# The FFN's entrance of an encoder layer: five instead of three pairs of gate and up tiles form their first four products ahead of the token sums

## The chip, the cores and the metric

The kernel runs on one core of a Trainium2 chip. The metric is the device time of one execution in microseconds (us), lower is better. A run's time is the median of several executions of the same program.

## The reference

One layer of a hybrid encoder on 1024 tokens of 1024 channels, float32 throughout. An attention group and a memory (mLSTM) group share an input and an output projection; then comes the feed-forward part (FFN), in which the change lies:

```python
    x = x + g1[:, None, :] * mix
    h = modulate(rms_norm(x, norm_ffn_g[l]), sh2, sc2)
    ffn = (jax.nn.silu(h @ w_gate[l]) * (h @ w_up[l])) @ w_down[l]
    x = x + g2[:, None, :] * ffn
return rms_norm(x, final_norm_g)
```

`w_gate` and `w_up` are 1024 x 2816, `w_down` is 2816 x 1024.

## The kernel before

**Products in split precision.** TensorE multiplies float32r operands, so each float32 operand is cut into a high part (ScalarE, ACT: a copy that rounds) and a low part (the rest, a subtraction on VectorE, DVE, or GpSimd, POOL). One product of a 128-row weight tile with a block of the tokens is four groups (`k`) of three matmuls each (`mm3`, L310): weight high with tokens high, weight high with tokens low, weight low with tokens high. All of them are 128x128 by 128x512. In the profile `whi` and `wlo` are the weight's parts, and `h110h`, `h213l`, `hT20h` and the like the tokens'; the low parts of the token sums overwrite tiles of the residual stream and are called `x` there.

**Seven products in place of eight.** The gate and up projections run by a scheme of the Strassen-Winograd kind. The hidden rows come in 11 pairs `p` (`NP`), and each pair has a gate tile (`i` = 0) and an up tile (`i` = 1). Weights and tokens are cut into 2 x 2 blocks. For each pair and each `i` there are seven products, named by what multiplies the tokens: `"11"`, `"21"`, `"22"`, `"T2"`, `"T3"`, `"T1"`, `"T4"`. Blocks `"11"` and `"21"` are the second half of the tokens as it is, normed. Block `"22"` is a block of the first half. The `T` blocks are **token sums**: chains of additions over all four blocks (`sums` in `norm2`, L1391), for four `k` each, almost all on DVE.

**What runs when.** `FF` is the order of units on TensorE:

```python
FF = [("b", p) for p in range(NB)] + [("v", 0)] + [("s", (p, i)) for p in range(1, NP - 1) for i in range(2)] + [("v", NP - 1)]
```

A unit `b` (`first_unit`, L1545) forms the first four products of pair `p`: `"11"` for gate and up, and `"21"` for gate and up. They need no token sums. A unit `v` (`pair_unit`, L1593) forms a pair's other ten products, gate and up in turn, with `"22"` first for pair 0. A unit `s` (`set_unit`, L1610) forms the other products of one tile: five where `p < NB`, and all seven where `p >= NB`. Before, units `b` stand for pairs 0, 1 and 2.

**What a product's bank is emptied by.** Each product fills one of the eight PSUM banks. The `"11"` product is copied out by ACT (`keep`, L1509). The `"21"` product is added to that copy by DVE (`c11`, L1526); for the gate tile a SiLU on ACT follows, for the up tile a multiplication on DVE (`post`, L1518) and a store. Their tiles come from `gu_tile` (L1498): pair 0 takes them from the rings `sg` and `su`, pairs 1 and 2 from tiles left over from the norm (`gsq`, `gssq`, `gv`, `gy`, and `gu`). For pair 2, `c11` also waits until the last mean has been multiplied in (`rs_used`).

**Weights.** A weight piece is loaded by a DMA from SyncE's queue (SP) into one of three `wst` tiles (`raw`, L442), then split; there are six `whi` and six `wlo` tiles (`wp`). Product n's end asks for piece n + 6 (`load_piece`, L487). Plain pieces of pair 0 have their low part made by DVE, those of later units `b` by POOL. The sums of weights for the other five products (`S1` to `S4`, and `A22`) come from raw tiles `wr` (three for each tile, `load_raws`, L1429) and one more `wst` (`load_last`, L1439). Their low part is DVE's for pair 0, POOL's for all others (`set_piece`, L1448). `load_last` for pair 0 is called in the unit `b` of pair `NB - 2`.

**Who sets the order.** The order of instructions on every engine is written out by a planner in the kernel (`Clock`), which runs its own estimate of the time. It lets a product start only when the bank taken eight allocations earlier has been given back in its own estimate (`slot`, L336); which bank the product really gets is settled later. The mean of the squares of the first token half takes one such bank (`ms`, L1342) and gives it back after eight multiplications with it (`normed`, L1364). The engines then work through their queues in that order, each waiting on semaphores.

Of the kernel before, what the change touches and what calls it, by code (L numbers as in the profile page):

```python
# [11 lines left out]
F32 = mybir.dt.float32  # L12
# [8 lines left out]
P = 128  # L21
# [3 lines left out]
HALF = 512  # L25
# [14 lines left out]
NX = 2  # L40
WARM = 4
PES = 3
NB = 3
KB = 5
AHEAD = 2
NP = NF // 2
# [2 lines left out]
MIX = [("o", i) for i in range(16)] + [("m", (i + 8) % 16) for i in range(16)]  # L49
FF = [("b", p) for p in range(NB)] + [("v", 0)] + [("s", (p, i)) for p in range(1, NP - 1) for i in range(2)] + [("v", NP - 1)]  # L50
SET = ["A11", "A12", "S2", "S3", "S1", "A22", "S4"]
# [198 lines left out]
def layer_kernel(ctx, tc, xT, c, w_ada, vecs, cons, rope, w_f, w_fT, w_t0, w_t, w_o, w_gu, w_d, out):  # L250
# [113 lines left out]
    with tc.manual_schedule():  # L364
# [41 lines left out]
        def set_w(p, i):  # L406
            return [("set", (p, i, m)) for m in SET if p >= NB or m not in ("A11", "A12")]

# [1030 lines left out]
        def load_last(s):  # L1439
            p, i = divmod(s, 2)  # L1440

            def arrived(t, delay):
                RAW[s]["12"][0] = t
                ck.chain(delay, lambda: None, flag=RAW[s]["12"][1])

            raw([P, 4, P], gate_w(p, i, 0, 1), sets_done[s], arrived)

        def set_piece(e, p, i, m):  # L1448
# [16 lines left out]
            else:  # L1465
                split(e, 0.0, lambda: R["12"][0], sh, s2_ok[s], R["12"][1], *done("A12"),
                      lambda: dve.tensor_sub(R["12"][0], R["12"][0], Q[2]), lo=eng)
            if len(set_p[s]) == (7 if p >= NB else 5):
                ck.chain(0.0, *set_p[s].values(), lambda: None, flag=sets_done[s])
# [17 lines left out]
        def prod(idx, m):  # L1487

            for k in range(4):
                yield [pieces[idx][2], hb_ok[m, k]] + ([slot("acc")] if k == 0 else [])  # L1490
                if k == 0:
                    bank = psum_tile([P, HALF], "acc")
                mm3(bank[0], weights(idx, k, 4), HB[m, k], k == 0, k == 3)
                ck.pe(0.65)
            load_piece()
            return bank

        def gu_tile(p, i, m):  # L1498
            if p == 2 and m in ("11", "12"):
                if i:  # L1500
                    return fp.tile([P, HALF], F32, name="gu")
                tag = "v" if m == "12" else "y"
                return NPL[0].tile([P, HALF], F32, tag=tag, name="g" + tag)
            if p == 1 and m in ("11", "12"):
                tag = "ssq" if i else "sq"
                return NPL[0].tile([P, HALF], F32, tag=tag, name="g" + tag, bufs=2 - i)
            return fp.tile([P, HALF], F32, tag=("sg", "su")[i], name=("sg", "su")[i], bufs=(6, 4)[i])

        def keep(p, i, X):  # L1509
            e = U[p, i] = [None, X[1]]  # L1510

            def copy():
                e[0] = gu_tile(p, i, "12")
                act.activation(e[0], X[0], AF.Copy)

            ck.chain(LAT, copy, flag=X[1])
# [9 lines left out]
        def c11(p, i, X):  # L1526
            u, u_ok = U[p, i]
            T = []

            def add():  # L1530
                T.append(fp.tile([P, HALF], F32, tag="tt", name="c11", bufs=4) if i else gu_tile(p, 0, "11"))
                dve.tensor_add(T[0], X[0], U[p, i][0])

            ck.chain(LAT, u_ok, *(rs_used if p == 2 else ()), add, flag=X[1])
            ck.chain(0.0, X[1], lambda: post(p, i, "11", T[0], FREE))
            if i:
                ck.chain(0.0, a_ok[p, "11"], lambda: store_act(p, "11", SG[p]["11"]))
            return X[1]
# [6 lines left out]
        def first_unit(p, w0):  # L1545
            for i in range(2):
                keep(p, i, (yield from prod(w0 + i, "11")))
            for i in range(2):
                if p == NB - 2:
                    load_last(i)  # L1550
                C11[p, i] = c11(p, i, (yield from prod(w0 + 2 + i, "21")))

        def set_steps(p, i):
# [3 lines left out]
            def add(out, a, b):  # L1557
                if out not in T:
                    T[out] = gu_tile(p, i, out)
                dve.tensor_add(T[out], a[0], T[b])  # L1560
# [32 lines left out]
        def pair_unit(p, w0):  # L1593

            if p >= NB:
                for i in range(2):
# [13 lines left out]
        def set_unit(pi, w0):  # L1610
            p, i = pi
            if p >= NB:
                keep(p, i, (yield from prod(w0, "11")))
# [609 lines left out]
        fp = ffpool.__enter__()  # L2223
# [90 lines left out]
```

## Time and profile before

| | us |
|---|---|
| median of 3 runs (lowest, highest) | 1393.42 (1390.51, 1393.83) |
| the profiled execution's own time | 1393.51 |
| its span, first to last instruction | 1391.7 |
| TensorE busy | 1289.2 (93%) |
| DVE busy | 1033.3 (74%) |
| ACT busy | 709.0 (51%) |
| POOL busy | 706.1 (51%) |

All times in the views count from the span's start. The stage around the change runs from about 714 us (first product of pair 0) to about 791 us (last product of `v` of pair 0). From there to 1160 us run the units of the other pairs, then the down projection. In the timeline a row is an instruction, or several alike merged: start, duration, engine, line, operation, output and inputs, count, and in brackets the idle time ahead of it with what ended it. Nearly all instructions of ACT, DVE and POOL have line L98, since one helper records them, so groups go by their tiles. Matmul durations overlap: the distance from start to start is what a matmul costs.

### The profile page before, as it was taken

Reading aid. Unit: us, or ns where it says so; the run is one execution under the profiler, and the core shown is the slowest. Engines: PE = TensorE matmul, PEld = TensorE weight load, DVE = VectorE, ACT = ScalarE, POOL = GpSimd, SP = SyncE. Lnnn points to the kernel's source line nnn. Section 1 sums busy time; section 2 is a strip of 40 time slices with the busy share of each in tenths; the row PEclk is TensorE's granted clock in tenths of the full one; section 3 lists DMA queues with packets and bytes.
Section 4 is the critical chain, followed back from the end, with each engine's and each line's share of the span. In section 5 each row is a group of like instructions: output and inputs, shape, how many; then the busy total and the mean of one; then the engine's idle time right before and its main releaser. Section 6 shows DMA issues by size and latency. Waiting matters only on the chain.

```text
span 1391.7 us, 19566 instructions
## 1 busy us (share of the span) xinstructions
PE 1289.2 (93%) x6588; PEld 1079.7 (78%) x6596; DVE 1033.3 (74%) x1536; ACT 709.0 (51%) x1335; POOL 706.1 (51%) x584
## 2 busy tenths in 40 slices
PE   7898888899999979989997899999999999979997
PEld 5786677888778978777776788888888887857887
DVE  6936698975789747758689886766676654998866
ACT  6575366778577755454477333332333334344462
POOL 0344677655656525677512265554554545445542
PEclk9999999999999999999999899999999999989999
DMA  9444433233233235663652343233332259733324
GB/s 355 158 129 118 114 103 95 84 99 105 65 108 97 67 131 180 201 225 102 198 187 89 105 138 106 99 107 106 114 114 81 76 178 328 288 79 103 95 64 155
DMA packets 103892, 185.98 MB, mean 134 GB/s; under 512 B 11504, under 2 KB 33136, under 8 KB 103792
## 3 DMA queue, kind: packets, MB, share of 16 engines
q1 hardware_dynamic: 90400, 162.63, 36.8%
q10 hardware_dynamic: 13392, 22.10, 4.2%
q8 instruction: 52, 0.85, 0.2%
q14 instruction: 48, 0.39, 0.1%
HBM read 137.76 MB, written 43.25 MB: 130 GB/s over the span
## 4 chain that ended last, share of the span: by engine, by line
PE 55%; DVE 18%; issue 8%; DMA 6%; ACT 5%; POOL 5%; SPq 1%; DVEq 0%; POOLq 0%; ACTq 0%
PE acc L311 15%; PE acc L312 15%; PE acc L313 15%; DVE sst L98 3%; DVE y L98 2%; DVE PT L98 2%; PE av L1209 2%; DVE x L98 2%; PE T L1190 2%; POOL wlo L98 2%; PE S L1158 1%; SPq L316 1%; DMA x<-in_xT_dram 1%; PE acct L313 1%; DVE s L98 1%
## 5 line engine op out<-in xcount | busy, mean ns | idle before, releaser
L98 POOL TENSOR_TENSOR wlo<-wst,whi 128x512 fp32r<-128x512 f32 (+2 forms) x187 | 264.5, 1420 | 262.3 <-ACT whi L98 236.4
L98 ACT ACTIVATE whi<-wst 128x512 fp32r<-128x512 f32 (+2 forms) x219 | 131.0, 605 | 110.2 <-PE acc L313 34.2
L312 PE MATMUL acc<-x,whi 128*128 128x512 f32 x352 | 138.4, 393 | 5.9 <-DVE x L98 5.9
L98 POOL TENSOR_SCALAR P<-P,sst 128x1024 f32<-128x1024 f32 x64 | 85.1, 1330 | 88.1 <-DVE sst L98 64.3
L98 POOL TENSOR_TENSOR wlo<-wr,whi 128x512 fp32r<-128x512 f32 x56 | 77.4, 1383 | 76.9 <-ACT whi L98 75.5
L311 PE MATMUL acc<-hh,whi 128*128 128x512 f32 x224 | 97.8, 436 | 6.5 <-ACT xp L98 5.3
L311 PE MATMUL acc<-whi,wch 128*128 128x512 f32 x244 | 96.5, 395 | 6.1 <-ACT wch L98 6.1
L313 PE MATMUL acc<-whi,wcl 128*128 128x512 f32 x244 | 96.8, 397 | 2.9 <-DVE wcl L98 2.8
L312 PE MATMUL acc<-wlo,wch 128*128 128x512 f32 x244 | 96.1, 394 | 0.1
L98 ACT ACTIVATE P<-S,sst,colq 128x1024 f32<-128x1024 f32 x64 | 77.2, 1207 | 36.8 <-DVE sst L98 26.9
L98 ACT ACTIVATE whi<-wr 128x512 fp32r<-128x512 f32 x60 | 37.9, 632 | 107.5 <-DVE wr L98 50.1
L98 DVE TENSOR_TENSOR PT<-T,PT 128x512 fp32r<-128x512 f32 x128 | 83.3, 681 | 10.7 <-ACT PT L98 10.5
L312 PE MATMUL acc<-hl,whi 128*128 128x512 f32 x224 | 90.9, 406 | 0.0
L313 PE MATMUL acc<-hh,wlo 128*128 128x512 f32 x224 | 90.8, 405 | 0.0
L98 POOL TENSOR_TENSOR wlo<-s,whi 128x512 fp32r<-128x512 f32 x40 | 54.0, 1352 | 67.5 <-ACT whi L98 67.5
L1190 PE MATMUL T<-ident,P 128*128 128x128 f32 x512 | 72.8, 280 | 15.9 <-DVE PT L98 9.3
L98 DVE TENSOR_TENSOR sg<-acc,sg 128x512 f32<-128x512 f32 x67 | 45.4, 687 | 55.8 <-PE acc L313 55.5
L311 PE MATMUL acct<-whi,hh 128*128 128x256 f32 (+1 forms) x256 | 82.8, 324 | 4.2 <-ACT hh L98 2.8
L98 ACT ACTIVATE PT<-T 128x512 fp32r<-128x512 f32 x128 | 71.8, 596 | 28.5 <-PE T L1190 27.8
L98 DVE TENSOR_REDUCE sst<-S 128x1 f32<-128x1024 f32 x64 | 77.7, 1214 | 11.4 <-PE S L1158 9.9
L312 PEld LDWEIGHTS acc<-x,whi 128*128 128x128 f32 x352 | 66.5, 189 | 21.0 <-DVE x L98 7.3
L98 POOL TENSOR_TENSOR ada<-ada,cond 128x512 f32<-128x512 f32 x48 | 69.2, 1443 | 23.3 <-DMA ada<-in_w_ada_dram 23.2
(478 smaller groups left out, 3859.6 us busy)
## 6 DMA issues: line engine op xcount, KB each, us to landing
wr<-in_w_gu_dram SPq DMA_DIRECT2D x66, 256.0 KB, 2.7
ada<-in_w_ada_dram SPq DMA_DIRECT2D x64, 256.0 KB, 3.2
wd<-in_w_d_dram SPq DMA_DIRECT2D x22, 512.0 KB, 6.4
wst<-in_w_gu_dram SPq DMA_DIRECT2D x34, 256.0 KB, 3.1
wst<-act_d SPq DMA_DIRECT2D x33, 256.0 KB, 4.1
ada<-in_w_ada_dram SPq DMA_DIRECT2D x16, 512.0 KB, 7.1
wst<-in_w_o_dram SPq DMA_DIRECT2D x32, 256.0 KB, 3.9
act_d<-sg ACTq DMA_DIRECT2D x31, 256.0 KB, 2.2
```

Source lines behind the costliest of these rows:

```text
L98: return fn(*args, **kw)
L311: nc.tensor.matmul(acc, w[0], x[0], start=first, stop=False)
L312: nc.tensor.matmul(acc, w[0], x[1], start=False, stop=False)
L313: nc.tensor.matmul(acc, w[1], x[0], start=False, stop=last)
L316: (q or nc.sync).dma_start(dst, src)
L1158: nc.tensor.matmul(sp[:, halves(n)], qs[:, j * P:(j + 1) * P], k2[g][m][:, halves(n)], start=m == 0, stop=m == 1)
L1190: nc.tensor.transpose(tp[:, k], Pt[q][:, (4 * b + k) * P:(4 * b + k + 1) * P], ident)
L1209: nc.tensor.matmul(av, va[:, k, h // 4], PT[it][m][:, k], start=(k, m) == (0, 0), stop=(k, m) == (NJ - 1, 1))
```

## The change

`NB` goes from 3 to 5, so units `b` stand for pairs 0 to 4, and the units `s` of pairs 3 and 4 form five products instead of seven. The `"11"` and `"21"` products of pairs 3 and 4 (eight products) move ahead of the unit `v` of pair 0, with their loads, splits, copies, additions, SiLUs, multiplications and stores. Eight new tiles of 128x512 float32, one for each of these products, hold the results until pairs 3 and 4 come up. The two `load_last` calls for pair 0 move from pair 1's unit to pair 3's. The weights of these eight products are loaded as plain pieces, in addition to the raw tiles that the sums need; the pieces `A11` and `A12` of the four sets fall away.

```diff
-NB = 3
+NB = 5
...
             if p == 1 and m in ("11", "12"):
                 tag = "ssq" if i else "sq"
                 return NPL[0].tile([P, HALF], F32, tag=tag, name="g" + tag, bufs=2 - i)
+            if 2 < p < NB and m in ("11", "12"):
+                return fp.tile([P, HALF], F32, name=f"gu{p}{i}{m}")
             return fp.tile([P, HALF], F32, tag=("sg", "su")[i], name=("sg", "su")[i], bufs=(6, 4)[i])
```

## The prediction

> **What bounds the kernel now.** I read the page's shares first, then a table of windows, then TensorE's timeline where that table shows a hole, then the queues of DVE, POOL and ACT around it.
>
> ```profile
> PE 1289.2 (93%) x6588; PEld 1079.7 (78%) x6596; DVE 1033.3 (74%) x1536; ACT 709.0 (51%) x1335; POOL 706.1 (51%) x584
> 740.00:760.00 20.00, 16.28 (x70) 12.62 (x68) 19.30 (x32) 12.76 (x23) 1.83 (x1) 0.99 0.26 81
> 760.00:780.00 20.00, 13.02 (x42) 9.40 (x43) 17.73 (x30) 9.86 (x18) 0.00 (x0) 0.67 0.15 53
> 780.00:800.00 20.00, 20.00 (x90) 16.57 (x89) 18.49 (x25) 5.46 (x10) 9.18 (x6) 1.00 0.38 125
> 791.00:1160.00 369.00, 369.00 (x1629) 305.54 (x1629) 252.71 (x297) 118.59 (x192) 189.85 (x137) 1.00 0.35 119
> ```
>
> The columns are the window, then busy time and count of TensorE, its weight loads, DVE, ACT and POOL, then granted clock, DMA share and GB/s. TensorE is the bound: from 791 to 1160 us it is never idle. Between 740 and 780 it is not: it issues 70 and 42 matmuls where a full window has 90, and its clock falls to 0.67. There DVE is busy 19.30 and 17.73 of 20 us while POOL does almost nothing.
>
> ```profile
> 746.04 0.39 PE L311 MATMUL acc<-h210h,whi 128*128 128x512 f32 x1
> 748.76 0.39 PE L311 MATMUL acc<-h220h,whi 128*128 128x512 f32 x1
> 754.20 0.39 PE L311 MATMUL acc<-hT20h,whi 128*128 128x512 f32 x1
> 756.12 0.50 PE L311 MATMUL acc<-hT21h,whi 128*128 128x512 f32 x1 [1.07 <-ACT hT21h L98]
> 758.36 0.50 PE L312 MATMUL acc<-x,whi 128*128 128x512 f32 x1 [1.74 <-DVE x L98]
> 760.93 0.80 PE L311 MATMUL acc<-hT22h,whi 128*128 128x512 f32 x1 [1.83 <-ACT hT22h L98]
> 763.77 0.80 PE L312 MATMUL acc<-x,whi 128*128 128x512 f32 x1 [2.04 <-DVE x L98]
> 766.84 0.80 PE L311 MATMUL acc<-hT23h,whi 128*128 128x512 f32 x1 [1.85 <-ACT hT23h L98]
> 769.79 0.79 PE L312 MATMUL acc<-x,whi 128*128 128x512 f32 x1 [2.15 <-DVE x L98]
> 774.71 0.39 PE L311 MATMUL acc<-hT30h,whi 128*128 128x512 f32 x1
> ```
>
> Pair 2's last early product starts at 746.04, pair 0's two `"22"` products follow at 748.76, and at 754.20 the first `"T2"` product starts and then waits for each token sum. Twenty-four matmuls from 748.76 to 754.20 give 0.2267 us each, so a product of 12 costs 2.72. The next 24 should end at 754.20 + 5.44 = 759.64, but `"T3"` starts at 774.71. **The hole is 15.07 us**: the six bracketed waits are 10.68, and the remaining 4.4 is the lowered clock, so an idle microsecond here costs about 1.4.
>
> **The change, part by part.**
>
> *TensorE.* Eight products move ahead of 748.76: 8 x 2.72 = 21.76 us. As much goes from the units of pairs 3 and 4, where TensorE is full, so moving costs and gains nothing by itself. It gains what it fills of the hole. `"T2"` would then start at 754.20 + 21.76 = 775.96, and its eleventh matmul, which needs the low part of the fourth sum, comes 10 x 0.2267 later, at 778.23. Before, that part was ready for the matmul of 769.79. The cover is 8.5 us, and all now depends on how much later DVE gets there.
>
> *DVE: what leaves the sums' stretch.* Product n asks for weight piece n + 6, so pair 0's sums of weights are asked for eight products later.
>
> ```profile
> L98 DVE TENSOR_TENSOR wlo<-s,whi 128x512 fp32r<-128x512 f32 x3 | 2.0, 679 | 0.0
> L98 DVE TENSOR_TENSOR wr<-wr 128x512 f32<-128x512 f32 x2 | 1.4, 679 | 0.0
> L98 DVE TENSOR_TENSOR wlo<-wr,whi 128x512 fp32r<-128x512 f32 x2 | 1.4, 678 | 0.0
> L98 DVE TENSOR_TENSOR wlo<-wst,whi 128x512 fp32r<-128x512 f32 x2 | 1.3, 678 | 0.0
> 758.83 0.67 DVE L98 TENSOR_TENSOR x<-x,ms 128x512 f32<-128x512 f32 x1
> 759.43 0.68 DVE L98 TENSOR_TENSOR x<-x,x 128x512 f32<-128x512 f32 x1
> 764.84 0.68 DVE L98 TENSOR_TENSOR wlo<-s,whi 128x512 fp32r<-128x512 f32 x1
> 769.06 0.68 DVE L98 TENSOR_TENSOR x<-t,hT23h 128x512 fp32r<-128x512 f32 x1
> ```
>
> The first four rows are DVE's groups from 742.8 to 759.5: nine instructions of pair 0's weight sums, which stand 0.60 us from start to start (758.83 to 759.43). They leave, 5.4 us, and so does the one at 764.84: 6.0 in all before the last low part of `"T2"` (769.06, ready at 769.74). What comes in: two additions and a multiplication of pair 3 (1.8), and the first two weight sums' subtractions and low parts (2.4), which fall after 759.5. The net is -1.8.
>
> *POOL's low parts, and what they do to DVE.* The plain pieces of pairs 3 and 4 have their low part made on POOL, in the stretch where POOL now idles.
>
> ```profile
> L98 POOL TENSOR_TENSOR wlo<-wst,whi 128x512 fp32r<-128x512 f32 x8 | 12.1, 1526 | 39.6 <-ACT whi L98 39.0 <-PE acc L312 0.6
> 724.59 3.49 POOL L98 TENSOR_TENSOR wlo<-wst,whi 128x512 fp32r<-128x512 f32 x2 [33.00 <-ACT whi L98]
> 724.56 2.35 DVE L98 TENSOR_TENSOR s<-s,wr 128x512 f32<-128x512 f32 x2
> 722.76 1.29 DVE L98 TENSOR_TENSOR s<-wr 128x512 f32<-128x512 f32 x2
> 735.11 2.74 POOL L98 TENSOR_TENSOR wlo<-wst,whi 128x512 fp32r<-128x512 f32 x2 [0.58 <-PE acc L312]
> 736.68 2.47 DVE L98 TENSOR_TENSOR x<-x,ms 128x512 f32<-128x512 f32 x4
> L98 DVE TENSOR_TENSOR sg<-su,sg x31: 677/1639/1661, 787.4 to 1152.8; 128x512 f32<-128x512 f32 x31
> ```
>
> Eight such pieces (pairs 1 and 2) took 12.1 us of POOL, 1.53 each. Beside them two DVE additions of SBUF with SBUF took 2.35 us, against 1.29 for two without it (722.76); the multiplications with the mean, which lies in PSUM, kept 2.47 for four. The last row gives the price: 0.677 us undisturbed, 1.639 as a rule where POOL is at work, so 0.96 per POOL instruction that meets one. The sums are nearly all SBUF with SBUF. Eight new POOL pieces cost the sums 8 x 0.96 = 7.7 us; the bounds are 0 (POOL falls into gaps) and 12.2 (each holds DVE for its whole length). I take 7.7, as it is the median of the nearest row.
>
> The Trainium skill, SBUF — State Buffer, section "Who interferes with whom", says that a DVE instruction with two SBUF inputs and a GpSimd one that reads SBUF exclude each other for a whole instruction, while one with a PSUM input isn't touched; the rows just shown agree. By this rule the sum would be the upper bound, 12.2, if POOL always came first; the first rival below is that case.
>
> The last part of `"T2"` is then ready at 769.74 - 1.8 + 7.7 = 775.6, ahead of 778.23: **the hole closes**, with 2.6 us to spare.
>
> *A new wait: the late pieces.* The mean's bank is given back after the multiplication at 758.83, so at 759.5; call this M. The planner, which counts banks eight back, holds a product there: before, pair 0's second `"22"`; after, pair 3's second `"11"`, since the eight banks count to it now. On the chip nothing waits there (the product at 751.48 in the old order ran before M), but pieces that are asked for later stand in ACT's and POOL's queues behind the sums.
>
> ```profile
> 762.49 0.61 ACT L98 ACTIVATE whi<-s 128x512 fp32r<-128x512 f32 x1
> wst<-in_w_gu_dram SPq DMA_DIRECT2D x34, 256.0 KB, 3.1
> ```
>
> Before, the piece asked for one product after M (759.5 + 2.72 = 762.2) had its high part at 762.49 and its low part ready at 765.52 (the 764.84 row), M + 6.0. After, that place is pair 4's last piece. M itself moves by -5.4 and by seven POOL pieces, + 6.7, to 760.8. The piece is ready between M + 6.0 = 766.8 and, if its 3.1 us transfer also falls there, 769.9; TensorE wants its low part at 748.76 + 7 x 2.72 + 2 x 0.2267 = 768.25. The first weight sum, asked for a product later and with a subtraction more (0.60), is ready at 770.1 to 773.2, wanted at 770.97. The wait is 0 to 2.2 us. I take **2.0**, near the top, since the queues' order carries the planned transfer.
>
> *What I cost at nothing.* ACT gets eight splits, four copies and two SiLUs in the stretch, at most 14 x 0.6 = 8.4 us; from 740 to 780 it is busy 22.6 of 40; its two stores more are only issued there. SP gets eight transfers of 256 KB, 2.1 MB; DMA share is 0.26 and 0.15 there. The two `load_last` keep their distance to the unit that reads them. If either were late, it would add to the same wait, not beside it. Banks: pair 2's two sums wait for M with the mean, which leaves five for the new products; a sixth would start at 762.4, by when all three are about free. Pairs 3 and 4 go from seven to five products a tile:
>
> ```profile
> 802.00:856.00 54.00, 54.00 (x240) 44.72 (x239) 43.32 (x50) 16.90 (x28) 31.51 (x23) 1.00 0.39 132
> 860.00:936.00 76.00, 76.00 (x337) 62.94 (x336) 50.10 (x61) 24.76 (x40) 38.74 (x28) 1.00 0.31 104
> ```
>
> Pairs 1 and 2 (first row) already run so, TensorE full and DVE at 43.32 of 54, 80%; pairs of seven products (second row) have DVE at 66%. Without that fifth of slack, DVE's backlog from the entrance would reach TensorE through the banks.
>
> *Sum:* 1393.5 (the profiled execution's own 1393.51; the median is 1393.42) - 15.1 + 2.0 = **1380.4**.
>
> **The rivals.**
>
> *POOL's pieces cost DVE their whole length.* Holding is then 12.2 and M is 759.5 - 5.4 + 7 x 1.53 = 764.8; pair 4's last piece comes at M + 9.1 = 773.9, 5.7 late, and with the clock's 1.4 that is 8.0: 1393.5 - 15.1 + 8.0 = 1386.4. For it: the stretch is DVE's fullest. Against it: the row's median is 0.96.
>
> *The new additions stand ahead of the sums.* If pair 4's two additions were queued before the end of `"T2"`'s sums, DVE would wait for that pair's last product, until 748.76 + 21.76 = 770.5, and the sums from 759.43 on (10.3 us) would follow: ready at 782.0 with the two additions, 3.8 late, x 1.4 = 5.3, so 1383.7. Against it: the planner's hold at M puts them late.
>
> *The gain is given back at the down projection.* The eight tiles change what the down projection's tiles are laid over.
>
> ```profile
> 1160.00:1260.00 100.00, 90.34 (x373) 70.47 (x373) 80.38 (x89) 44.90 (x77) 50.30 (x36) 0.95 0.63 219
> 1164.96 0.69 DVE L98 TENSOR_TENSOR wcl<-wd,wch 128x512 fp32r<-128x512 f32 x1 [9.74 <-DMA wst<-act_d]
> ```
>
> TensorE loses time there already (373 of 441 matmuls). If the wait of 9.74 grew by as much again and fell on TensorE, 9.74 x 1.4 = 13.6 would go: 1394.0, no change. Against it: these tiles are free long before.
>
> *Slower: holding runs through all the sums.* From 742.8 to 769.74 stay some 30 DVE instructions of SBUF with SBUF. If each were held by 0.96, `"T2"` would be ready at 769.74 - 1.8 + 28.8 = 796.7, 18.5 late, x 1.4 = 25.9: 1404.3. It decides from 24 us of holding on (about 25 held instructions), which takes `"T2"` to 792. Against it: eight POOL instructions of 1.53 can hold no more than 12.2.
>
> **How the numbers follow.** About 0.3% (4.2 us) is what a measurement can tell from no change. Chances: the forecast (1377 to 1383) 0.62, POOL's whole length 0.24, additions ahead 0.05, given back 0.04, slower 0.05. The first three are faster: 0.91; same 0.04; slower 0.05. The range is from 1377 (no wait, and about a microsecond more from the calmer clock) to 1388 (the second case with a little more), about 0.9 of the chance.
>
> **What would show it.** TensorE's row of windows from 740 to 780 shows 85 to 90 matmuls each and a clock near 1.00. Eight POOL pieces stand between 743 and 770. DVE's SBUF additions there show durations up to 1.7. `"T2"` starts at about 778, and its waits are gone. A wait of about 2 us, for ACT, POOL or DVE weight pieces, stands ahead of pair 4's last product or the first `"22"`. Pairs 3 and 4 take 27.2 us each instead of 38.1, with TensorE full. Wrong would be: waits for `hT2` parts still there (POOL), waits for banks, a hole between 800 and 910, or a longer one after 1145.

## The result and the profile after

| | before | changed kernel |
|---|---|---|
| median (lowest to highest), us | 1393.14 (1390.51 to 1393.83) | 1381.31 (1380.33 to 1382.95) |
| ratio to before, 95% interval | | 0.9929 (0.9911 to 0.9946) |
| profiled execution, its span, us | 1393.51, 1391.7 | 1381.44, 1379.7 |

The change takes 11.8 us off, against 13.1 forecast (1380.4). The windows of the changed kernel, columns as in the prediction, show TensorE's hole smaller, with 90 and 68 matmuls from 740 to 780 in place of 70 and 42, and its clock at 1.00 throughout, while DVE is busy for all of the 20 us from 760 to 780:

```profile
740.00:760.00 20.00, 20.00 (x90) 16.54 (x89) 18.06 (x22) 13.08 (x24) 10.05 (x7) 1.00 0.28 93
760.00:780.00 20.00, 16.14 (x68) 11.99 (x67) 20.00 (x33) 13.58 (x26) 3.36 (x2) 1.00 0.21 65
780.00:800.00 20.00, 20.00 (x90) 16.58 (x89) 18.27 (x27) 6.41 (x11) 5.46 (x4) 1.00 0.47 146
802.00:910.00 108.00, 108.00 (x478) 89.48 (x477) 94.67 (x107) 31.95 (x53) 59.32 (x41) 1.00 0.39 130
```

TensorE's timeline of the changed kernel, with the start of pair 0, the start of pair 1's first `"21"` product (730.51), every wait marked up to the first product with the `"T1"` sums, and that product:

```profile
712.39 0.39 PE L311 MATMUL acc<-h110h,whi 128*128 128x512 f32 x1
724.49 0.50 PE L313 MATMUL acc<-h110h,wlo 128*128 128x512 f32 x1 [0.27 <-POOL wlo L98]
730.51 0.39 PE L311 MATMUL acc<-h210h,whi 128*128 128x512 f32 x1
767.71 0.51 PE L313 MATMUL acc<-h210h,wlo 128*128 128x512 f32 x1 [1.11 <-POOL wlo L98]
773.07 0.50 PE L313 MATMUL acc<-h220h,wlo 128*128 128x512 f32 x1 [2.15 <-DVE wlo L98]
776.68 0.50 PE L313 MATMUL acc<-h220h,wlo 128*128 128x512 f32 x1 [0.60 <-DVE wlo L98]
779.08 0.39 PE L311 MATMUL acc<-hT20h,whi 128*128 128x512 f32 x1
789.96 0.39 PE L311 MATMUL acc<-hT10h,whi 128*128 128x512 f32 x1
```

The six waits for `"T2"` parts are gone. Three new ones stand where the prediction looked for one: at pair 4's last product and at both `"22"` products, for low parts of weights. The same places of the stage before, and the one wait ahead of those that the prediction shows, were:

```profile
713.60 0.39 PE L311 MATMUL acc<-h110h,whi 128*128 128x512 f32 x1
726.43 0.50 PE L313 MATMUL acc<-h110h,wlo 128*128 128x512 f32 x1 [1.00 <-POOL wlo L98]
732.44 0.39 PE L311 MATMUL acc<-h210h,whi 128*128 128x512 f32 x1
780.16 0.39 PE L311 MATMUL acc<-hT10h,whi 128*128 128x512 f32 x1
```

**The yardstick.** I call *entrance* the time from pair 0's first matmul to the first `"T1"` matmul, less 2.72 us for each early product beyond those of before. Before it is 780.16 - 713.60 = 66.6 us; after it is 789.96 - 712.39 - 8 x 2.72 = 55.8. Without any wait it would be 216 matmuls of 0.2267 and about 0.9 for the mean, 49.9. It leaves out what runs ahead of the stage: over all runs below, pair 0 starts between 707.0 and 713.6 us. Both programs give the engines the same instructions in the same order up to there, so that spread belongs to neither. Of the 12.0 us between the two spans, 10.8 are the entrance and 1.2 lie ahead of it.

The entrance still holds one wait that no edit here aims at: TensorE's wait for a low part in pair 1's first product. It is 1.00 us before and 0.27 in the changed kernel; over all profiles it is 1.0 in four (before, plain low parts on DVE, four pairs, the first T2-first run) and at most 0.3 in the others. So a second number, *lost*, counts behind it: the time from pair 1's first `"21"` product to the first `"T1"` product, less 2.72 us for each of the products between (12 before, 16 with four pairs, 20 with five). Before it is 780.16 - 732.44 - 12 x 2.72 = 15.1, the prediction's hole; after it is 789.96 - 730.51 - 20 x 2.72 = 5.1. **By these two profiles the change itself gained 10.0 us of the 12.0**; 0.7 are pair 1's wait, 1.2 the earlier start.

### The profile page after: what moved, and what is told of

It is laid out like the page before. It is cut to its first block, busy times and chain, and to the rows that moved or that the text cites. A ratio compares the mean times of both kernels' runs of the same rounds, so it can differ in the third digit from the quotient of the medians.

```text
span 1379.7 us, 19583 instructions
## 1 busy us (share of the span) xinstructions
PE 1286.5 (93%) x6596; PEld 1079.1 (78%) x6596; DVE 1044.1 (76%) x1536; ACT 707.0 (51%) x1335; POOL 706.7 (51%) x584
## 4 chain that ended last, share of the span: by engine, by line
PE 53%; DVE 20%; issue 9%; DMA 6%; ACT 5%; POOL 5%; SPq 1%; DVEq 0%; ACTq 0%; POOLq 0%
PE acc L311 14%; PE acc L313 14%; PE acc L312 14%; DVE sst L98 3%; DVE y L98 3%; DVE x L98 3%; DVE PT L98 2%; PE av L1209 2%; PE T L1190 2%; PE S L1158 1%; POOL wlo L98 1%; SPq L316 1%; DMA x<-in_xT_dram 1%; DVE s L98 1%; DVE wd L98 1%
## 5 line engine op out<-in xcount | busy, mean ns | idle before, releaser
L98 POOL TENSOR_TENSOR wlo<-wst,whi 128x512 fp32r<-128x512 f32 (+2 forms) x191 | 269.2, 1416 | 276.5 <-ACT whi L98 255.1
L98 POOL TENSOR_TENSOR wlo<-wr,whi 128x512 fp32r<-128x512 f32 x52 | 72.1, 1387 | 71.8 <-ACT whi L98 68.9
L1190 PEld LDWEIGHTS T<-ident,P 128*128 128x128 f32 x512 | 59.4, 143 | 26.7 <-POOL P L98 9.9
L98 POOL TENSOR_TENSOR wlo<-s,whi 128x512 fp32r<-128x512 f32 x40 | 55.1, 1378 | 48.1 <-ACT whi L98 48.0
L98 DVE TENSOR_TENSOR wcl<-wd,wch 128x512 fp32r<-128x512 f32 x50 | 50.7, 1027 | 36.9 <-ACT wch L98 27.4
```

What stands on the lines that cost most here:

```text
L98: return fn(*args, **kw)
L1190: nc.tensor.transpose(tp[:, k], Pt[q][:, (4 * b + k) * P:(4 * b + k + 1) * P], ident)
```

## The experiments

All are the changed kernel with one edit (the last with two), but for one that starts from before. They ran in four sets, each beside runs of before of its own, whose medians were 1393.14 (the first two rows), 1391.25 (mean's bank, pair 0's low parts on POOL, plain low parts on DVE, four pairs), 1391.51 (the changed kernel again, the two single runs, T2 first) and 1389.18 (the last two rows). So ratios can be compared across the table, medians only within a set. Entrance and lost come from one profile each.

| kernel | entrance to T1, us | lost, us | median, us | ratio to before, 95% interval |
|---|---|---|---|---|
| before | 66.6 | 15.1 | 1393.14 | |
| changed kernel | 55.8 | 5.1 | 1381.31 | 0.9929 (0.9911 to 0.9946) |
| changed kernel, again | 56.4 | 5.7 | 1379.32 | 0.9917 (0.9887 to 0.9947) |
| mean's bank not counted | 56.4 | 5.8 | 1380.08 | 0.9920 (0.9901 to 0.9939) |
| pair 0's low parts on POOL | 57.4 | 6.7 | 1380.29 | 0.9924 (0.9900 to 0.9949) |
| plain low parts on DVE | 55.5 | 3.8 | 1378.87 | 0.9905 (0.9888 to 0.9921) |
| four pairs | 62.7 | 10.8 | 1386.56 | 0.9971 (0.9957 to 0.9986) |
| plain low parts left out | 50.6 | 0.0 | 1371.07 (one run) | |
| before, pair 0's low parts on POOL | 70.7 | 20.0 | 1395.55 (one run) | |
| T2 first | 52.8 | 1.2 | 1375.95 | 0.9893 (0.9861 to 0.9924) |
| T2 first, again | 53.3 | 2.6 | 1378.12 | 0.9929 (0.9910 to 0.9949) |
| T2 first, plain low parts on DVE | 52.5 | 1.8 | 1377.05 | 0.9914 (0.9897 to 0.9931) |

Four expectations (mean's bank, pair 0's low parts on POOL, plain low parts on DVE, four pairs) still measure the entrance to the first `"T3"` matmul. It is 61.1 before and 50.4 in the changed kernel that way, and came out at 51.0, 52.0, 50.1 and 57.3.

**Is it the late asking?** The prediction put the new wait down to the planner's count of banks. In this kernel the first half's mean is taken out of that count:

```diff
                     ms, held[n] = psum_tile([P, HALF], "ms")
+                    if n == 0 and then is norm2:
+                        PP["ring"]["acc"].pop()
```

> Five pairs, but the planner no longer counts the first half's mean among the eight banks, so its own estimate does not stop at pair 3's second product and the later weight pieces are asked for earlier. Measure: the entrance, from the first matmul of pair 0's first product to the first matmul with the T3 sums, less 2.72 us for each early product more than before; 61.1 us before, 50.4 with five pairs, 44.4 if nothing waited. Theory 'order' (what is left of the loss comes from the late asking): the three waits for low parts (1.11, 2.15, 0.60 us) go, the T2 sums come up to 5 us later but stay within their cover of 8.5 us; entrance 45 to 47, time 1377 to 1379. Rival 'DVE is full': the weight sums' ten DVE instructions go back among the token sums, T2 gets late, waits for T2 parts of 3 to 6 us replace the waits removed; entrance 50 to 54, time 1381 to 1385.

The windows row, TensorE's one wait, and the first weight sum's subtraction and low part on DVE:

```profile
740.00:780.00 40.00, 36.15 (x152) 29.43 (x152) 39.97 (x57) 25.69 (x47) 12.01 (x8) 0.96 0.28 86
764.23 0.68 DVE L98 TENSOR_TENSOR wst<-wst,s 128x512 f32<-128x512 f32 x1
769.64 0.68 DVE L98 TENSOR_TENSOR wlo<-wst,whi 128x512 fp32r<-128x512 f32 x1
770.38 0.53 PE L313 MATMUL acc<-h220h,wlo 128*128 128x512 f32 x1 [3.85 <-DVE wlo L98]
```

The asking did come earlier: pair 0 starts at 709.79 here, so the subtraction comes 54.4 us after it, against 56.3 in the changed kernel (its 768.73 row is below), and pair 4's last product no longer waits. But the low part comes 59.9 us after it, as before the edit (772.34 - 712.39 = 60.0). DVE is busy for 39.97 of 40 us, and what was asked for sooner queued for longer. The three waits merged into one of 3.85, and the entrance stayed. My theory of the order of asking falls as the cause of the loss; it set only where the loss showed. The rival that DVE is full had the size right (51.0 of 50 to 54), but not the place: no `"T2"` part came late.

**What a POOL piece costs DVE.** Three kernels move low parts between the two engines.

```diff
# pair 0's low parts on POOL
-            eng = dve if p == 0 else gps
+            eng = gps
# plain low parts of pairs 3 and 4 on DVE
-                  lo=dve if specs[i][3:] == (1,) or i < 9 or start["m", 2] <= i < start["b", 1] else None)
+                  lo=dve if specs[i][3:] == (1,) or i < 9 or start["m", 2] <= i < start["b", 1] or start["b", 3] <= i < start["v", 0] else None)
```

> Five pairs, with the low parts of pair 0's ten weight sums on POOL instead of DVE. Theory 'DVE is full at the weight sums': POOL is idle from 767.7 to 790.3, so these low parts come 1 to 2 us earlier, the waits of 2.15 and 0.60 for them shrink to under 1 together; the entrance goes from 50.4 to about 48.5, time about 1379.5. Rival 'each POOL piece costs DVE 0.6 to 1.1 us, as much as the 0.60 it saves': DVE is no earlier, the subtraction ahead of each split is as late as before and the entrance stays within 1 us of 50.4, time 1380.5 to 1382.

> Five pairs, with the low parts of the plain pieces of pairs 3 and 4 on DVE instead of POOL. Theory 'POOL holds DVE': in the changed kernel the eight POOL pieces lengthened seven DVE instructions by 6.2 us in all; on DVE they cost 8 x 0.60 = 4.8 us and no DVE instruction between 742 and 770 is longer than 0.75; the entrance stays within 1.5 us of 50.4 and the time within 1380 to 1382.5. Rival 'POOL's work is nearly free for DVE': 4.8 us more on a full engine, the waits for low parts grow by 3 to 5 us, time 1384 to 1387.

> Three pairs as before, with the low parts of pair 0's ten weight sums on POOL instead of DVE. Theory 'each POOL piece costs DVE 0.78 to 0.96 us where it saves 0.60': eight of the ten lie ahead of the end of T2's sums, so these end 1.4 to 2.9 us later and the hole grows, the entrance to T1 goes from 66.6 to 68.5 to 70.5, time 1395 to 1397. Rival 'work taken from DVE is gained': 4.8 us less on DVE, the hole shrinks by 4.8 to 6.7, entrance 60 to 62, time about 1387.

First the changed kernel itself: POOL's low parts from 743 on, and all DVE instructions of the stretch that took longer than 0.75 us.

```profile
743.09 1.30 POOL L98 TENSOR_TENSOR wlo<-wst,whi 128x512 fp32r<-128x512 f32 x1 [0.64 <-ACT whi L98]
745.13 1.30 POOL L98 TENSOR_TENSOR wlo<-wst,whi 128x512 fp32r<-128x512 f32 x1 [0.74 <-ACT whi L98]
747.89 4.86 POOL L98 TENSOR_TENSOR wlo<-wst,whi 128x512 fp32r<-128x512 f32 x3 [1.46 <-ACT whi L98]
758.07 1.30 POOL L98 TENSOR_TENSOR wlo<-wst,whi 128x512 fp32r<-128x512 f32 x1 [5.32 <-ACT whi L98]
760.68 1.60 POOL L98 TENSOR_TENSOR wlo<-wst,whi 128x512 fp32r<-128x512 f32 x1 [1.31 <-ACT whi L98]
765.89 1.76 POOL L98 TENSOR_TENSOR wlo<-wst,whi 128x512 fp32r<-128x512 f32 x1 [3.62 <-ACT whi L98]
743.25 1.69 DVE L98 TENSOR_TENSOR t<-x,x 128x512 f32<-128x512 f32 x1
745.46 1.52 DVE L98 TENSOR_TENSOR h221l<-x,h221h 128x512 fp32r<-128x512 f32 x1
748.11 1.79 DVE L98 TENSOR_TENSOR h222l<-x,h222h 128x512 fp32r<-128x512 f32 x1
749.82 1.78 DVE L98 TENSOR_TENSOR h223l<-x,h223h 128x512 fp32r<-128x512 f32 x1
751.52 1.77 DVE L98 TENSOR_TENSOR x<-x,x 128x512 f32<-128x512 f32 x1
758.63 1.29 DVE L98 TENSOR_TENSOR x<-x,x 128x512 f32<-128x512 f32 x1
767.05 1.15 DVE L98 TENSOR_TENSOR x<-x,x 128x512 f32<-128x512 f32 x1
```

Each long one lies on a POOL piece and ends about 0.55 us after it (743.09 + 1.30 = 744.39, and 743.25 + 1.69 = 744.94). Their excess over 0.68 adds up to 6.2 us, 0.78 for each of the eight pieces. The piece at 760.68 lengthened no DVE instruction. With these low parts on DVE the same stretch reads:

```profile
L98 DVE TENSOR_TENSOR wlo<-wst,whi 128x512 fp32r<-128x512 f32 x8 | 5.4, 680 | 0.0
L98 DVE TENSOR_TENSOR x<-x,x 128x512 f32<-128x512 f32 x7 | 4.8, 681 | 0.0
740.00:780.00 40.00, 38.05 (x161) 31.00 (x160) 39.73 (x67) 26.40 (x49) 0.19 (x1) 0.96 0.28 87
```

Eight low parts stand on DVE in the stretch of the first two rows (one of them a weight sum's), every addition takes 0.68, POOL is all but silent, and the entrance is 55.5. By the lost time, 3.8 against 5.1 and 5.7, DVE fares 1.3 to 1.9 us better when it makes the eight low parts itself, close to the 8 x (0.78 - 0.60) = 1.4 that the two prices give; one profile is thin evidence for so little. The median, 1378.87, came out below the 1380 to 1382.5 expected.

The other way round, pair 0's ten on POOL gained nothing in the changed kernel: 57.4, and 6.7 lost. Both expectations missed there, as the entrance to T3 grew by 1.6 us where it was to shrink or stay within 1. In the kernel before it made the hole larger, 70.7 against 66.6 and 20.0 lost against 15.1, a little over what was expected; the last low part of `"T2"` starts 59.4 us after pair 0 there, against 55.5. That the single time of that kernel is longer proves nothing, as the eight runs of before beside it went from 1384.79 to 1395.65. An idle POOL was no free help here.

**Less work for DVE.** In this kernel the low parts of the eight plain pieces of pairs 3 and 4 are made by no engine:

```diff
+            if lo == "none":
+                def one():
+                    split_hi()
+                    p[1] = p[0]
+                ck.chain(delay, *before, one, flag=p[2])
+                return
             ck.chain(delay, *before, split_hi, split_lo, flag=p[2])
...
-                  lo=dve if specs[i][3:] == (1,) or i < 9 or start["m", 2] <= i < start["b", 1] else None)
+                  lo="none" if start["b", 3] <= i < start["v", 0] else dve if specs[i][3:] == (1,) or i < 9 or start["m", 2] <= i < start["b", 1] else None)
```

> The changed kernel without the low parts of the eight plain weight pieces of pairs 3 and 4: the third matmul of those products takes the high part again, so neither POOL nor DVE makes these low parts. Theory 'DVE is full, and POOL's pieces hold it': 6.2 us of holding are gone, the token sums and pair 0's weight sums come that much earlier, the waits for low parts at the first two '22' products nearly vanish; the entrance to T1 falls from 55.8 to 50.5 to 52, time about 1376 to 1378. Rival 'the late asking': pieces are asked for where they were, the waits stay, entrance 55 to 56.

```profile
740.00:780.00 40.00, 40.00 (x178) 33.12 (x177) 37.68 (x63) 24.59 (x45) 0.29 (x1) 1.00 0.35 112
```

TensorE is never idle from 740 to 780, DVE has 2.3 us to spare, and the entrance is 50.6, within a microsecond of the 49.9 without waits. The 6.2 us of holding taken away came back as 5.2 us of entrance, though the pieces were asked for where they had been. One of the waits, the 1.11 at pair 4's last product, goes by construction, since its low part is left out. But the kernel with these low parts on DVE doesn't have that wait either; it differs by 4.8 us of DVE's time and lost 3.8 at the `"22"` products, where nothing is lost here. So what the changed kernel still loses is DVE's time ahead of pair 0's weight sums, not the asking. The time of 1371.07, under the 1376 to 1378 expected, is one run, and its pair 0 starts at 707.0, the earliest of all.

**Half the dose.** `NB = 4`.

> Four pairs instead of five form their first four products early: half the dose. Four products are 10.9 us of the hole of 15.1. Theory 'the hole is filled as far as products are there, and what is left is late T2 sums': T2's last part is ready at about 770.4 on the clock of before and wanted at 767.4, about 3 us late, with the lowered clock 4; no waits for weight pieces; entrance about 50, time about 1382. Rival 'five pairs already lose a part to late pieces, so fewer are better': T2 late by less than 1 us, entrance 46 to 48, time 1378 to 1380. Rival 'linear in the dose': gain half of 11.8, time 1387.

TensorE's waits in it for the last `"T2"` sum, and that sum's low part on DVE:

```profile
771.31 0.50 PE L311 MATMUL acc<-hT23h,whi 128*128 128x512 f32 x1 [2.68 <-ACT hT23h L98]
775.46 0.79 PE L312 MATMUL acc<-x,whi 128*128 128x512 f32 x1 [3.65 <-DVE x L98]
774.73 0.67 DVE L98 TENSOR_TENSOR x<-t,hT23h 128x512 fp32r<-128x512 f32 x1
```

The theory and the first rival missed: the entrance is 62.7, a gain of 3.9 us where the dose is 10.9 and I had expected some 11. The rival that the gain goes with the dose isn't excluded by the clock: the medians differ by 4.7 us, with 1.9 to 6.0 by the interval, against half of 11.8. By the profile it is somewhat less than half (15.1 - 10.8 = 4.3 of 10.0). Pair 0 starts at 712.54 here and 713.60 before, so the last `"T2"` sum's low part starts 62.2 us after it, against 55.5 before: 6.7 us later. Here most of the weight sums' DVE work still stands ahead of it (eleven such instructions from 754.9 to 774.2), and the holding by four POOL pieces and the additions of pair 3 come on top. With five pairs only one (768.73) stands ahead of it. So five pairs gain not only by more products: their eight products push these weight sums behind the token sums.

**A better order.** With five pairs, `"22"` first no longer fills a hole, and its first weight sum needs a transfer, a subtraction and a low part, the latter two on DVE. Here pair 0 takes the order of the last pair's unit `v` (the expectation calls it that of the other pairs, but their units `s` put `"22"` last):

```diff
-            for m in ("T2", "T3", "22", "T1", "T4") if p else ("22", "T2", "T3", "T1", "T4"):
+            for m in ("T2", "T3", "22", "T1", "T4"):
...
-            order = ("A11", "A12", "S2", "S3", "S4", "S1", "A22") if p else ("S4", "S2", "S3", "S1", "A22")
+            order = ("A11", "A12", "S2", "S3", "S4", "S1", "A22") if p else ("S2", "S3", "S4", "S1", "A22")
```

> The changed kernel once more, unchanged, beside the other kernels of this set on the same chip. All theories: the entrance as in its first profile within 1 us (from pair 0's first matmul to the first T1 matmul, less 2.72 us per early product more than before: 55.8 us; 66.6 before), time 1379 to 1382. A difference of over 1 us in the time with the same entrance is the spread of what runs ahead of the stage.

> Five pairs, with pair 0's later products in the order of the other pairs (T2, T3, 22, T1, T4 instead of 22, T2, T3, T1, T4) and its weight pieces asked for in that order. The first piece needed then wants no transfer and no subtraction, and the one that does has four products more time. Theory 'what is left is the chain of three DVE steps of the first weight sum through a full queue': the waits at the '22' products go, T2's first weight sum and its last token sum come about when wanted; entrance to T1 52 to 54, time 1377 to 1379.5. Rival 'DVE's total work is the bound whatever the order': the wait moves to a T2 or T3 product, entrance 55 to 57, time 1380 to 1383.

> Five pairs with pair 0's later products in the order T2, T3, 22, T1, T4, unchanged from its first run, for a narrower interval. Entrance to T1 within 1 us of 52.75, time 3 to 4 us under the changed kernel's, about 1376 to 1378, ratio to before 0.988 to 0.990. If its lead was the spread of what runs ahead of the stage, the entrance is the same but the ratio goes to 0.992.

> As the run beside it, with the low parts of the plain pieces of pairs 3 and 4 on DVE instead of POOL. Theory 'DVE is full; a POOL piece costs it 0.78 us, a low part of its own 0.60': DVE gains 8 x 0.18 = 1.4 us over the entrance, entrance to T1 51 to 53, time at most 1.5 us shorter. Rival 'once the order is right, DVE no longer binds': no difference within 0.5 us. Rival 'low parts in DVE's queue come later for TensorE than POOL's': new waits for them at pairs 3 and 4, entrance 54 to 56.

The first T2-first run's row, and its one marked wait after pair 1:

```profile
740.00:780.00 40.00, 39.48 (x173) 31.89 (x172) 40.00 (x57) 25.16 (x46) 11.50 (x8) 1.00 0.31 99
773.43 0.50 PE L313 MATMUL acc<-hT30h,wlo 128*128 128x512 f32 x1 [0.52 <-DVE wlo L98]
```

The changed kernel, run again, came out as expected (56.4, 1379.32). With T2 first DVE is as full as ever, but TensorE gets 173 matmuls in 40 us. Two runs give an entrance of 52.8 and 53.3, against 55.8 and 56.4 for the changed kernel, so about 3 us, and lost are 1.2 and 2.6 against 5.1 and 5.7. With the plain low parts on DVE as well it is 52.5, with 1.8 lost, between the two T2-first runs: nothing more is shown by it. The order matters where the total doesn't change, and the rival that DVE's total alone decides falls too. In the times this is not settled: beside each other the medians were 1379.32 and 1375.95, but the repeat came out at a ratio of 0.9929 (0.9910 to 0.9949), the changed kernel's own and not the 0.988 to 0.990 expected. Three microseconds are 0.2%, and these intervals are wider. T2 first is the better order by its profile in both runs; that it is faster by the clock isn't shown.

## Why the prediction was right, and where its steps were off

- **The hole closes.** Right. The late T2 sums were the bound, the eight products covered them, and their six waits vanished. The last part of `"T2"` was forecast for 775.6 on the clock of before. It was made by the DVE instruction at 770.53, so it was ready at 771.21 + 1.21 (the later start of pair 0 before) = 772.4. Most of the difference is the order in DVE's queue: the forecast put seven new instructions of pair 3 and the weight sums ahead of it, and three stood there (766.45, 768.73 and 769.93, shown below).
- **What POOL does to DVE.** Right in kind, sized at 7.7, measured 6.2: one of the eight pieces lengthened nothing. The first rival, POOL's whole length (12.2), fell.
- **Where the mean's bank is given back (M).** Forecast 760.8; the multiplication at 758.03 ended at 758.70, which is 759.9 on that clock.
- **The new wait.** This is the term that was mis-sized. Its place was right, at pair 4's last piece and the first weight sum. Its size was 2.0, with 2.2 as the upper bound; measured are three waits of 3.86 us together, and with the slower matmuls around them 5.1 us lost, two and a half times the term. (The entrance's 55.8 - 49.9 = 5.9 has 0.9 more, from ahead of pair 1's first `"21"` product.) The sign of 85 to 90 matmuls in 20 us held from 740 to 760 (90), not from 760 to 780 (68). The step that failed is "ready at 770.1 to 773.2" for the first weight sum: it came at 773.02, 774.2 on that clock. With M at 759.9 that is 14.3 us behind M, where I had 9.3 to 12.4. I had read the delay from one piece of before, 6.0 us, and added a transfer and one subtraction; in the changed kernel more DVE work stands between, and DVE is busy for all of 760 to 780:

```profile
758.03 0.68 DVE L98 TENSOR_TENSOR x<-x,ms 128x512 f32<-128x512 f32 x1
766.45 0.68 DVE L98 TENSOR_TENSOR gu<-acc,gu 128x512 f32<-128x512 f32 x1
768.73 0.68 DVE L98 TENSOR_TENSOR wst<-wst,s 128x512 f32<-128x512 f32 x1
769.93 0.68 DVE L98 TENSOR_TENSOR c<-acc,gu 128x512 f32<-128x512 f32 x1
770.53 0.68 DVE L98 TENSOR_TENSOR x<-t,hT23h 128x512 fp32r<-128x512 f32 x1
772.34 0.68 DVE L98 TENSOR_TENSOR wlo<-wst,whi 128x512 fp32r<-128x512 f32 x1
```

  From the subtraction to the end of the low part 4.3 us pass, of which 1.4 are the two instructions; the rest is the split's high part and other DVE work ahead. And I took the lateness of two pieces as one wait, the larger; in fact the second `"22"` product's piece was later still and added its own.
- **The cause I gave for it**, that the pieces are asked for late, behind M, doesn't set the size. In the first experiment the subtraction came 1.9 us earlier and the low part at the same time; what sets it is DVE's work ahead of the low parts and their order.
- **The clock's share.** I put the 4.4 us that the hole had beyond its six waits down to the lowered clock. In the changed kernel three waits of 3.86 us cost 5.1, 1.3 for one, with a granted clock of 1.00 in every window, so not all of the 4.4 need be the clock; the factor of 1.4 itself served.
- **Pairs 3 and 4 at five products.** Right: from 802 to 910 TensorE is busy for 108.00 of 108 us, and DVE takes 94.67, 88%, more than the 80% of pairs 1 and 2 before, but still under the full.
- **The down projection.** Right: nothing was given back. (The new tiles are six, not eight, since the sum of an up tile's `"21"` product goes to a tile of a ring, `c` in the views.) The distance from T1 to the first down matmul with `wch` is 384.7 before (1164.9 - 780.16) and 363.3 after (1153.3 - 789.96), 21.4 us less, about the eight products moved (21.76); from T1 to the end of the span it is 21.8 less:

```profile
L311 PE MATMUL acc<-whi,wch x244: 387/389/795, 1164.9 to 1345.0; 128*128 128x512 f32 x122
L311 PE MATMUL acc<-whi,wch x244: 387/389/793, 1153.3 to 1332.9; 128*128 128x512 f32 x122
```

- **The total** came out closer than its parts deserve, and that is luck: the change itself gained 10.0 and not 13.1, and 1.9 us of the 12.0 between the two profiles are pair 1's old wait and the earlier start of pair 0.

## What to carry to other kernels

When work is pulled forward to cover a wait, count what the pulled work does to the engine that causes the wait, with the time for which another engine's work holds it, and what it pushes behind. Read a queue's delay from a stretch in which that queue is as full as it will be; asking earlier moved the place of a wait here and not its size, as DVE had no gap. When the cover is there, look again at orders that were chosen to fill the old hole.

## What the runs showed of the hardware that was not expected

- The price of a low part to DVE was no lower when POOL made it (0.78 us in the mean, up to 1.1) than when DVE did (0.60): moving ten of them to POOL lengthened the entrance by 4.1 us in the kernel before, in its one profile.
- The start of this stage, after some 700 us of the same instructions in the same order, spread over 1.2 us between the two first profiles, and over 6.6 us (707.0 to 713.6) in all profiles.
